# A two-layer fp32 trunk: where the compression weights lie, and in what order the first row tile's attention and the last projections run

## The chip, the cores and the metric

The kernel runs on one core of one Trainium2 chip. The metric is the device time of one execution in microseconds; the time of a kernel is the median of its runs.

## The reference

The input is one sequence of 256 rows with 1024 columns. Two layers follow each other, each of the form `x <- x + RMSNorm_post(mixer(RMSNorm_pre(x)))`. The first mixer is gated linear attention; the change does not touch it. The second is native sparse attention. Cut to what matters here:

```python
p = h @ w_in                       # q 1024, kc, vc, ks, vs, kw, vw 256 each, gates 48, z 1024
q, kc, ks, kw = rope(q), rope(kc), rope(ks), rope(kw)
flat = blocks_of_32_rows(kc or vc) + pe             # 15 overlapping blocks per group
kcmp = silu(flat_k @ ck_w1) @ ck_w2                 # (2048 -> 256 -> 64), the compression
vcmp = silu(flat_v @ cv_w1) @ cv_w2
o = sigmoid(gl + b_gate) * [softmax(q kcmp) vcmp, softmax(q ks) vs, softmax(q kw) vw]
y = (sum of the three) * silu(z) @ w_out
```

There are 16 heads in 4 groups of 4, with 64 columns each. With 256 rows the selection takes every block and the window covers every row, so both those branches are causal attention over all rows.

## The kernel before

**Tiles and precision.** The 256 rows are two row tiles, t = 0 and t = 1, of 128. A projection's weights come in a `Chunk` of 512 (or 280) columns: `load` fetches it in four pieces of 256 rows by 512 columns into buffers named `raw`, of which there are four, and `split` makes of each piece a high part `hi` (ScalarE, line 190) and a low part `lo` (line 196, on VectorE or on GpSimd by a table). A product `mm3` is then three matmuls (lines 211 to 213): high by high, low by high, high by low. The activations are split in the same way into `hT`.

**The second layer, in the order written.** `kc_part(t)` and `ks_part(t)` project kc with vc and ks with vs; the kc side goes through `rope` (VectorE lines 823 and 825, then a GpSimd sum that writes each head twice, `dup`, line 832), is transposed on TensorE and lands in `kcT` (line 850). Line 885 adds the position vectors `vT` to `kcT` and writes `flat`, the compression's input: eight additions, four for kc and four for vc, each one group with all sixteen row positions. `vT` itself is the transpose of `vecs`, made at line 815 before the first `kc_part`. The compression's first weight has eight pieces `w1`, pieces 0 and 1 in the tile later used for z, and pieces 2 to 7 each in a `raw` buffer. `hidden(u)` (lines 891 to 895) runs the eight products of pieces 2u and 2u+1 into one PSUM bank, `o`; in the trace they stand at line 894. The window part kw, vw and the gates are two chunks of 280 columns, `ch_kw[0]` and `ch_kw[1]`. After the fourth `hidden`, silu (`hid`), two transposes, the second compression weight (lines 1175 and 1179), columns 256 to 272 of `kTh`/`kTl` (the compressed keys) and the block matrix `vblk` (line 1186, four pieces) follow.

**Queries, gates and attention.** `q_steps(p, t)` projects half p of the queries for one row tile and ends with `rope`; `q_T` transposes the result into a `qS` tile, of which there are six. `z_steps(p)` projects half p of z, transposed, into two `acc` banks. A `Unit(g, t)` is the attention of group g for row tile t: `scores` (line 1001, scale and row minimum on VectorE at line 1006, exp on ScalarE at line 1008), `values` (transposes of P at line 1074, copies `pT`, products with vs and vw at line 1088, the compressed part through `pcT` at lines 1094 to 1112), and `finish`, which multiplies with the gate and z. `out_steps(t)` is the output projection of a row tile. In row tile 1 a unit has twice the columns.

**What sets the order.** All loads go through one queue in the order written (line 125). The matmuls of projections follow each other on TensorE in the order written (`chain`), and a scheduler places the rest between them by its own model; the pace given to `split` and the numbers `PA[..]` only tell that scheduler beside which matmul a split is to stand. PSUM has two `acc` banks, three `s`, two `t` and one `o`.

In `before` the order after kw is: q(0,0), hidden(2), q_T(0,0), q(0,1), hidden(3), compression's end, q_T(0,1), q(1,0), q(1,1), units (0,0) and (1,0), z(0), unit (2,0), z(1), unit (3,0), out_steps(0), the four units of row tile 1, out_steps(1).

Of the kernel before, what the change touches and what calls it, by code (L numbers as in the profile page):

```python
# [16 lines left out]
P = 128  # L17
# [70 lines left out]
def hybrid_kernel(ctx: ExitStack, tc: tile.TileContext, x, positions, pre_norm, post_norm,  # L88
# [725 lines left out]
    b = bank()  # L814
    nc.tensor.transpose(b[:, :32], vecs, ident[:32, :32])
    nc.vector.tensor_copy(vT, b[:, :32])
# [50 lines left out]
    def load_w1(u0, u1):  # L867
        first = lp.tile([P, 2, 4, CHID], F32, tag="zT", name="w1_0") if u0 == 0 else None
        for u in range(u0, u1):
            raw = wp.tile([P, 4, CHID], F32, tag="raw", name=nm("w1"), bufs=N_RAW) if first is None else first[:, u]  # L870
            src = (nsa_ck_w1, nsa_cv_w1)[u % 2]
            dma(raw, src[0, (u // 2) * 512:(u // 2 + 1) * 512, :].rearrange("(k p) n -> p k n", p=P))
            w1.append(raw)
# [5 lines left out]
    ch_kw[0].load()  # L879
    kc_part(1)  # L880
    for kv in range(2):
# [9 lines left out]
    def hidden(u):  # L891
        for j in range(u * 4, u * 4 + 4):
            for kv in range(2):
                nc.tensor.matmul(hid_b[kv * 64:(kv + 1) * 64, :CHID], flat[:, j, kv].rearrange("p g c -> p (g c)"),  # L894
                                 w1[u * 2 + kv][:, j % 4, :], start=(j == 0), stop=(j == 15))

    ch_kw[0].split((ch_ks, PA[6]))
    for t in range(NT):
        o = proj(ch_kw[0], hT, t)
        nc.scalar.activation(vw_sb[:, t, :24], o[:, 256:280], AF.Copy, scale=rs1[t])  # L900
        k_T(o, t, 272 + t * P)
    hidden(0)
    ch_kw[1].load().split((ch_kw[0], PA[7]))
    load_w1(2, 4)
# [9 lines left out]
    hidden(1)  # L914
# [233 lines left out]

    ch_q[0].load().split((ch_kw[1], PA[8]))
    load_w1(4, 6)  # L1150
    ch_q[1].load(0, 4)
    run(q_steps(0, 0))
    ch_q[1].split((ch_q[0], PA[9]))
    hidden(2)
    load_w1(6, 8)
    ch_q[1].load(4, 8).split((ch_q[0], PA[9]))
    q_T(0, 0)
    q01 = q_steps(0, 1)
    run(q01)
    hidden(3)  # L1160
# [28 lines left out]
    run(q01)  # L1189
# [9 lines left out]

    q_T(0, 1)  # L1200
    run(q_steps(1, 0))
    run(q_steps(1, 1))
    q_T(1, 0)
    unit(0, 0)
    q_T(1, 1)
    unit(1, 0)
    ch_z[0].load().split((ch_q[1], PA[10]))
    run(z_steps(0))
    for g in range(2):
        U[g, 0].finish()  # L1210
    unit(2, 0)
    ch_z[1].load().split((ch_z[0], PA[11]))
# [42 lines left out]
```

## Time and profile before

| | us |
|---|---|
| runs | 307.58, 305.57, 305.70 |
| median | 305.70 |
| profiled execution | 302.72 |
| its span | 300.8 |

The profile shows one execution. Its span runs from the first instruction to the last; the execution's own time is 1.92 us more. The busy time of an engine is the time in which it had an instruction under way: TensorE's matmuls are pipelined, so the length printed for one matmul is longer than the distance to the next. PE is TensorE, PEld its loading of weights, DVE VectorE, ACT ScalarE, POOL GpSimd. In a timeline "x8" counts instructions that stand together in a row, and the bracket at its end is the idle time of the engine just before, with what ended it. A product in fp32 is two passes in the trace, so the eight products of a `hidden` are sixteen matmul records. PEclk is the clock granted to TensorE, 1.00 for 2.4 GHz and 0.50 for 1.2 GHz.

### The profile page before, as it was taken

To read this page: it belongs to the slowest core of one execution; us is meant where nothing else is said; L and a number is where in the kernel's file an instruction comes from. 1 tells how busy PE (TensorE), PEld (TensorE's weight loads), DVE (VectorE), ACT (ScalarE), POOL (GpSimd) and SP (SyncE) were. 2 spreads that over 40 slices of the span, in tenths; PEclk is the share of its full clock that TensorE was granted. 3 is DMA by queue.
4 is the path that set the end of the run, shared out by engine and by line. 5 is a ranking of instruction groups with operands and counts; after the bars stand their busy time and mean duration, and the time that the engine had idled before them with its cause. 6 is when DMAs were issued, how large, how long until landed. Compare 5 with 4: busy or idle time off the path is not lost.

```text
span 300.8 us, 5374 instructions
## 1 busy us (share of the span) xinstructions
PE 286.6 (95%) x1788; PEld 239.7 (80%) x1788; DVE 215.3 (72%) x556; ACT 181.5 (60%) x468; POOL 167.0 (56%) x184
## 2 busy tenths in 40 slices
PE   7999999999999999889979999999997999999991
PEld 7888999999998887668958676899994678676660
DVE  1779569846979877576893536799999858877423
ACT  4896788667754757435534405679967637657301
POOL 1496968984383252927545035897799434172200
PEclk9999999999999999999999999999997799999998
DMA  7997588105677334394745785576144000100001
GB/s 214 403 362 217 151 258 288 56 22 186 204 220 212 92 82 130 64 289 147 195 162 144 274 263 180 190 218 232 42 142 139 2 0 0 71 2 0 2 0 71
DMA packets 28301, 44.57 MB, mean 148 GB/s; under 512 B 2865, under 2 KB 12513, under 8 KB 28274
## 3 DMA queue, kind: packets, MB, share of 16 engines
q1 hardware_dynamic: 28242, 44.23, 46.6%
q8 instruction: 14, 0.23, 0.3%
q14 instruction: 13, 0.11, 0.1%
q10 hardware_dynamic: 32, 0.01, 0.0%
HBM read 43.18 MB, written 1.05 MB: 147 GB/s over the span
## 4 chain that ended last, share of the span: by engine, by line
PE 63%; DVE 13%; issue 9%; POOL 6%; ACT 4%; DMA 3%; SPq 0%; POOLq 0%; DVEq 0%; ACTq 0%
PE acc L211 11%; PE acc L213 11%; PE acc L212 11%; PE s L468 4%; POOL lo L196 3%; PE s L212 3%; PE s L211 3%; PE s L213 3%; DVE lo L196 3%; PE o L894 3%; PE t L1074 3%; PE o L1088 3%; PE s L1001 2%; ACT hi L190 2%; DMA raw<-in_gla_w_in_dram 1%
## 5 line engine op out<-in xcount | busy, mean ns | idle before, releaser
L196 POOL TENSOR_TENSOR lo<-raw,hi 128x512 fp32r<-128x512 f32 (+2 forms) x63 | 82.8, 1334 | 44.4 <-ACT hi L190 44.4
L190 ACT ACTIVATE hi<-raw 128x512 fp32r<-128x512 f32 (+2 forms) x120 | 64.2, 583 | 37.7 <-DMA raw<-in_nsa_w_in_dram 26.6
L196 DVE TENSOR_TENSOR lo<-raw,hi 128x512 fp32r<-128x512 f32 (+2 forms) x57 | 53.6, 963 | 13.4 <-ACT hi L190 13.3
L1045 POOL TENSOR_SCALAR P<-P,cf 128x128 f32<-128x128 f32 (+1 forms) x64 | 29.2, 475 | 30.2 <-DVE cf L1041 14.4
L211 PE MATMUL acc<-hT,hi 128*128 128x256 f32 x160 | 45.2, 283 | 0.1
L212 PE MATMUL acc<-hT,hi 128*128 128x256 f32 x160 | 44.8, 280 | 0.0
L213 PE MATMUL acc<-hT,lo 128*128 128x256 f32 x160 | 44.5, 281 | 0.0
L211 PE MATMUL acc<-hi,hT 128*128 128x512 f32 (+2 forms) x112 | 39.2, 350 | 1.2 <-DVE yg L276 0.8
L213 PE MATMUL acc<-hi,hT 128*128 128x512 f32 (+2 forms) x112 | 38.9, 347 | 0.0
L212 PE MATMUL acc<-lo,hT 128*128 128x512 f32 (+2 forms) x112 | 38.8, 346 | 0.0
L1008 ACT ACTIVATE P<-P,mn 128x128 f32<-128x128 f32 (+1 forms) x64 | 28.4, 445 | 7.2 <-DVE mn L1006 5.9
L211 PEld LDWEIGHTS acc<-hT,hi 128*128 128x128 f32 x160 | 30.1, 188 | 0.4 <-DVE zT L362 0.3
L212 PEld LDWEIGHTS acc<-hT,hi 128*128 128x128 f32 x160 | 30.1, 188 | 0.1
L213 PEld LDWEIGHTS acc<-hT,lo 128*128 128x128 f32 x160 | 29.8, 188 | 0.0
L211 PEld LDWEIGHTS acc<-hi,hT 128*128 128x128 f32 x112 | 21.1, 188 | 5.3 <-ACT yg L269 1.2
L1006 DVE CUSTOM_DVE_ANT_0 P<-s,c 128x128 f32<-128x128 f32 (+1 forms) x64 | 20.6, 347 | 5.3 <-PE s L1001 4.4
L213 PEld LDWEIGHTS acc<-hi,hT 128*128 128x128 f32 x112 | 21.1, 188 | 2.9 <-DVE hT L311 0.4
L212 PEld LDWEIGHTS acc<-lo,hT 128*128 128x128 f32 x112 | 21.1, 188 | 2.0
L1074 PE MATMUL t<-c,P 128*128 128x128 f32 x96 | 17.4, 296 | 2.0 <-ACT pcT L1096 1.9
L440 POOL TENSOR_TENSOR lo<-raw,hi 128x512 fp32r<-128x512 f32 (+1 forms) x9 | 12.3, 1388 | 9.9 <-ACT hi L436 9.8
L1074 PEld LDWEIGHTS t<-c,P 128*128 128x128 f32 x96 | 11.1, 147 | 7.3 <-issue 3.6
L832 POOL TENSOR_TENSOR dup<-rt,rt 128x512 f32<-128x512 f32 x6 | 8.9, 1487 | 11.2 <-DVE rt L825 5.7
(268 smaller groups left out, 676.2 us busy)
## 6 DMA issues: line engine op xcount, KB each, us to landing
raw<-in_nsa_w_in_dram SPq DMA_DIRECT2D x24, 512.0 KB, 4.5
raw<-in_gla_w_in_dram SPq DMA_DIRECT2D x12, 512.0 KB, 6.1
raw<-in_gla_w_out_dram SPq DMA_DIRECT2D x8, 512.0 KB, 4.3
raw<-in_nsa_w_out_dram SPq DMA_DIRECT2D x8, 512.0 KB, 4.2
raw<-in_nsa_w_in_dram SPq DMA_DIRECT2D x8, 280.0 KB, 8.4
raw<-in_gla_w_in_dram SPq DMA_DIRECT2D x6, 344.0 KB, 3.4
home<-in_gla_w_in_dram SPq DMA_DIRECT2D x4, 512.0 KB, 6.7
w<-in_nsa_ck_w_dram SPq DMA_DIRECT2D x4, 512.0 KB, 3.8
```

What stands on the lines that cost most here:

```text
L190: m = after(nc.scalar.activation(hi[:, j, :n], raw[:, j, :n], AF.Copy), prev)
L196: eng.tensor_sub(lo[:, j, :n], raw[:, j, :n], f(hi[:, j, :n]))
L211: m = nc.tensor.matmul(o, a[0], b[0], start=start, stop=False, **kw)
L212: nc.tensor.matmul(o, a[0], b[1], start=False, stop=False, **kw)
L213: return m, nc.tensor.matmul(o, a[1], b[0], start=False, stop=stop, **kw)
L440: line(e, eng.tensor_sub(lo[:, j, :n], raw[:, j, :n], f(hi[:, j, :n])))
L468: m = nc.tensor.matmul(o[t][:, :chunk.n], hT[i][:, k, t * P:(t + 1) * P], w[j], start=(k == b == 0), stop=(k == KT - 1 and b == 2))
L894: nc.tensor.matmul(hid_b[kv * 64:(kv + 1) * 64, :CHID], flat[:, j, kv].rearrange("p g c -> p (g c)"), w1[u * 2 + kv][:, j % 4, :], start=( ...
L1006: nc.vector.tensor_tensor_reduce(out=o, in0=src, in1=masks[br], op0=ALU.add, op1=ALU.min, scale=-0.125, scalar=3.0e38, accum_out=self.mn[: ...
L1008: nc.scalar.activation(o, o, AF.Exp, scale=-1.0, bias=self.mn[:, j:j + 1], accum_out=self.sm[:, j:j + 1])
L1045: nc.gpsimd.tensor_scalar(o, o, cf[:, i * 2 + br:i * 2 + br + 1], 1.0, op0=ALU.mult, op1=ALU.mult)
L1074: pe(nc.tensor.transpose(b[:, i * P:(i + 1) * P], self.Pt[i][:, c0:c0 + P], ident))
```

## The change

The position vectors' transpose and copy move from before `kc_part(0)` to behind `kc_part(1)`. Pieces 2 to 7 of `w1` go into the six `qS` tiles, which are empty until the first `q_T`, and no longer into `raw`; so they are loaded ahead: pieces 2 and 3 before `kc_part(1)`, pieces 4 to 7 before the kw projections, together with `ch_kw[1]` and `ch_q[0]`. `hidden(1)` and `hidden(2)` follow the two row tiles of kw1, `hidden(3)` comes right after, and all their matmuls are now in the chain. The compression's end then lies beside q(0,0) and q(0,1). Behind it the order is: q(0,1), unit (0,0), z(0), unit (1,0), q(1,0), finish of both, q(1,1), unit (2,0), z(1), unit (3,0).

```diff
--- before.py
+++ after.py
@@ -811,9 +811,6 @@
     flat = cp.tile([P, 16, 2, GROUPS, 16], F32, tag="flat", name="flat")
     nc.gpsimd.memset(flat, 0.0)
     vT = cp.tile([P, 32], F32, tag="vT", name="vT")
-    b = bank()
-    nc.tensor.transpose(b[:, :32], vecs, ident[:32, :32])
-    nc.vector.tensor_copy(vT, b[:, :32])
 
     def rope(o, nh, t, twice):
 
@@ -865,9 +862,10 @@
     w1 = []
 
     def load_w1(u0, u1):
         first = lp.tile([P, 2, 4, CHID], F32, tag="zT", name="w1_0") if u0 == 0 else None
         for u in range(u0, u1):
-            raw = wp.tile([P, 4, CHID], F32, tag="raw", name=nm("w1"), bufs=N_RAW) if first is None else first[:, u]
+            raw = lp.tile([P, 4, CHID], F32, tag="qS", name=nm("w1"), bufs=6) if first is None else first[:, u]
             src = (nsa_ck_w1, nsa_cv_w1)[u % 2]
             dma(raw, src[0, (u // 2) * 512:(u // 2 + 1) * 512, :].rearrange("(k p) n -> p k n", p=P))
             w1.append(raw)
@@ -877,7 +875,11 @@
     ch_z = [Chunk(w_in, N_Z + p * 512, 512) for p in range(2)]
     load_w1(0, 2)
     ch_kw[0].load()
+    load_w1(2, 4)
     kc_part(1)
+    b = bank()
+    nc.tensor.transpose(b[:, :32], vecs, ident[:32, :32])
+    nc.vector.tensor_copy(vT, b[:, :32])
     for kv in range(2):
         kin = kcT[:, kv]
         for g in range(GROUPS):
@@ -891,17 +893,21 @@
     def hidden(u):
         for j in range(u * 4, u * 4 + 4):
             for kv in range(2):
-                nc.tensor.matmul(hid_b[kv * 64:(kv + 1) * 64, :CHID], flat[:, j, kv].rearrange("p g c -> p (g c)"),
-                                 w1[u * 2 + kv][:, j % 4, :], start=(j == 0), stop=(j == 15))
+                m = nc.tensor.matmul(hid_b[kv * 64:(kv + 1) * 64, :CHID], flat[:, j, kv].rearrange("p g c -> p (g c)"),
+                                     w1[u * 2 + kv][:, j % 4, :], start=(j == 0), stop=(j == 15))
+                chain(m, m)
 
     ch_kw[0].split((ch_ks, PA[6]))
+    ch_kw[1].load()
+    load_w1(4, 8)
+    ch_q[0].load()
     for t in range(NT):
         o = proj(ch_kw[0], hT, t)
         nc.scalar.activation(vw_sb[:, t, :24], o[:, 256:280], AF.Copy, scale=rs1[t])
         k_T(o, t, 272 + t * P)
+        if t == 0:
+            ch_kw[1].split((ch_kw[0], PA[7]))
     hidden(0)
-    ch_kw[1].load().split((ch_kw[0], PA[7]))
-    load_w1(2, 4)
     for t in range(NT):
         o = proj(ch_kw[1], hT, t)
         nc.scalar.activation(vw_sb[:, t, 24:], o[:, :232], AF.Copy, scale=rs1[t])
@@ -911,7 +917,10 @@
         nc.scalar.activation(g, g, AF.Exp, scale=-1.0)
         nc.vector.tensor_scalar(g, g, 2.0, 2.0, op0=ALU.mult, op1=ALU.add)
         nc.vector.reciprocal(g, g)
-    hidden(1)
+        hidden(t + 1)
+        if t == 0:
+            ch_q[0].split((ch_kw[1], PA[8]))
+    hidden(3)
 
 
 
@@ -1146,18 +1155,8 @@
             sl = slice(n * H, n * H + H)
             dma(out[0, t * P:(t + 1) * P, sl], X[:, t, sl])
 
-    ch_q[0].load().split((ch_kw[1], PA[8]))
-    load_w1(4, 6)
-    ch_q[1].load(0, 4)
-    run(q_steps(0, 0))
-    ch_q[1].split((ch_q[0], PA[9]))
-    hidden(2)
-    load_w1(6, 8)
-    ch_q[1].load(4, 8).split((ch_q[0], PA[9]))
-    q_T(0, 0)
-    q01 = q_steps(0, 1)
-    run(q01)
-    hidden(3)
+    q00 = q_steps(0, 0)
+    run(q00, 3)
     zT = lp.tile([P, KT, S], F32, tag="zT", name="zT2")
     hid = cp.tile([P, CHID], F32, tag="hid", name="hid")
     silu2(hid_b[:, :CHID], hid)
@@ -1186,7 +1185,8 @@
             nc.vector.tensor_tensor(vblk[:, 2 * p + G], b[rows, (p + 1) * 64:(p + 2) * 64].unsqueeze(1)
                                     .to_broadcast([64, 4, DH]),
                                     cc("blk")[rows].unsqueeze(2).to_broadcast([64, 4, DH]), op=ALU.mult)
-    run(q01)
+    run(q00)
+    q_T(0, 0)
     l2a.close()
     ap_ = ctx.enter_context(tc.tile_pool(name="l2b", bufs=1))
     ofT = [[lp.tile([P, KT, P], F32R, tag="qS", name=nm("ofT"), bufs=6) for n in "hl"] for t in range(NT)]
@@ -1197,19 +1197,21 @@
         run(U[g, t].scores())
         run(U[g, t].values())
 
+    ch_z[0].load().split((ch_q[0], 8))
+    run(q_steps(0, 1))
+    unit(0, 0)
     q_T(0, 1)
+    run(z_steps(0))
+    ch_q[1].load().split((ch_z[0], 0))
+    unit(1, 0)
     run(q_steps(1, 0))
-    run(q_steps(1, 1))
-    q_T(1, 0)
-    unit(0, 0)
-    q_T(1, 1)
-    unit(1, 0)
-    ch_z[0].load().split((ch_q[1], PA[10]))
-    run(z_steps(0))
     for g in range(2):
         U[g, 0].finish()
+    q_T(1, 0)
+    ch_z[1].load().split((ch_q[1], 0))
+    run(q_steps(1, 1))
     unit(2, 0)
-    ch_z[1].load().split((ch_z[0], PA[11]))
+    q_T(1, 1)
     run(z_steps(1))
     unit(3, 0)
     for g in range(2, 4):
```

The instructions' order on the engines, as the two programs have them, at three places.

VectorE around the additions `flat`, in the window projections; `lo` are splits of kw weights, `acc` is the bank of kw's first chunk, row tile 0, and `cos_t`, `sin_t` mark its rope. Before:

```order
L196 TENSOR_TENSOR lo_1939<-raw_1922,hi_1938 128x280
L850 COPY kcT<-t_1732 64x4x64
L850 COPY kcT<-t_1739 64x4x64
L885 TENSOR_TENSOR flat<-kcT,vT 128x16x15 x4
L196 TENSOR_TENSOR lo_1945<-raw_1924,hi_1944 128x280
L885 TENSOR_TENSOR flat<-kcT,vT 128x16x15 x4
L823 TENSOR_TENSOR rt_324_1856<-acc_1830,cos_t 128x256
L825 TENSOR_TENSOR rt_325_1857<-acc_1830,sin_t 128x4x32 x2
L338 COPY rb<-t_1795 128x256
```

And after:

```order
L196 TENSOR_TENSOR lo_1917<-raw_1840,hi_1916 128x280
L847 COPY kcT<-t_1733 64x4x64
L847 COPY kcT<-t_1740 64x4x64
L820 TENSOR_TENSOR rt_338_1884<-acc_1858,cos_t 128x256
L822 TENSOR_TENSOR rt_339_1885<-acc_1858,sin_t 128x4x32 x2
L882 COPY vT<-t_1747 128x32
L887 TENSOR_TENSOR flat<-kcT,vT 128x16x15 x8
L338 COPY rb<-t_1799 128x256
```

The rope of kw0's row tile 0 now stands ahead of the eight additions, and the copy `vT` between them, which waits for a transpose of TensorE.

That transpose and the first `hidden` on TensorE; `acc_1922` is kw0's row tile 1, `acc_1970` kw1's row tile 0, `dup_1789` belongs to ks. After:

```order
L211 MATMUL acc_1922<-hi_1828,hT_1317 128x280
L881 MATMUL t_1747<-c_64,vecs 128x32
L212 MATMUL acc_1922<-lo_1829,hT_1317 128x280
L213 MATMUL acc_1922<-hi_1828,hT_1318 128x280
L836 MATMUL t_1791<-c_64,dup_1789 128x128 x4
L211 MATMUL acc_1922<-hi_1828,hT_1317 128x280
L212 MATMUL acc_1922<-lo_1829,hT_1317 128x280
L213 MATMUL acc_1922<-hi_1828,hT_1318 128x280
L337 MATMUL t_1799<-dg_1803,onesr 128x256
L337 MATMUL t_1799<-dg_1804,onesr 128x256
L896 MATMUL o_1798<-w_0_1684,flat 64x256 x8
L211 MATMUL acc_1970<-hi_1898,hT_1317 128x280
```

Before the change line 894 stood at the same place, behind the same projection, and the transpose of `vecs` ahead of the layer's first projection.

TensorE at the end of q(0,1) and the start of the next projection; `t_2195` and `t_2101` are the bank with the compressed keys and values, `acc_2309`, `acc_2310` the two banks of z(0), and `acc_2185` the bank of q(0,1), whose buffer `acc_2310` takes over. Before:

```order
L211 MATMUL s_2257<-hi_2122,hT_1317 128x512
L1175 MATMUL t_2195<-hidT,w_1580 128x64 x2
L1179 MATMUL t_2195<-w_1580,hidR 128x64 x4
L963 MATMUL t_2216<-c_64,rt_384_2169 128x128 x4
L212 MATMUL s_2257<-lo_2123,hT_1317 128x512
...
L213 MATMUL s_2257<-hi_2128,hT_1318 128x512
L211 MATMUL acc_2506<-hT_1317,hi_2482 128x256
```

And after:

```order
L212 MATMUL acc_2185<-lo_2027,hT_1317 128x512
L1174 MATMUL t_2101<-hidT,w_1580 128x64 x2
L1178 MATMUL t_2101<-w_1580,hidR 128x64 x4
L213 MATMUL acc_2185<-hi_2026,hT_1318 128x512
L211 MATMUL acc_2185<-hi_2026,hT_1317 128x512
L212 MATMUL acc_2185<-lo_2027,hT_1317 128x512
L213 MATMUL acc_2185<-hi_2026,hT_1318 128x512
L211 MATMUL acc_2309<-hT_1317,hi_2161 128x256
...
L972 MATMUL t_2135<-c_64,rt_369_2129 128x128 x4
...
L211 MATMUL acc_2310<-hT_1317,hi_2161 128x256
```

VectorE at that place, after:

```order
L296 TENSOR_TENSOR kTl<-t_2101,kTh 128x4x16
L1185 TENSOR_TENSOR vblk<-t_2101,c_65 64x256 x4
L820 TENSOR_TENSOR rt_390_2210<-acc_2185,cos_t 128x512
L822 TENSOR_TENSOR rt_391_2211<-acc_2185,sin_t 128x8x32 x2
```

Before, the bank of q(0,1) was an `s` bank; now it is the `acc` bank that z(0) needs six of its matmuls and four transposes after the end of q(0,1), and its rope stands behind `kTl` and the four `vblk`.

TensorE after the last matmul of z(1) (the first row in both pieces); `P` are the probabilities, `s` the score banks, `acc_2996` is the first bank of out_steps(0). Before:

```order
L213 MATMUL acc_2736<-hT_1317,lo_2730 128x256
L1001 MATMUL s_2846<-kTh,qS_2293 128x272
...
L1074 MATMUL t_2457<-c_64,P_2395 128x128 x2
L1074 MATMUL t_2457<-c_64,P_2418 128x128 x2
L1088 MATMUL o_2022<-pT_2455,vs_sb 64x256 x2
L1094 MATMUL t_2466<-c_64,cS_2393 64x128
L1074 MATMUL t_2679<-c_64,P_2624 128x128 x2
...
L1088 MATMUL o_2022<-pT_2462,vw_sb 64x256 x2
L1112 MATMUL o_2022<-pcT_2468,vblk 128x128 x2
...
L211 MATMUL acc_2996<-hi_2934,ofT_2212 128x512
```

And after:

```order
L213 MATMUL acc_2736<-hT_1317,lo_2606 128x256
L1010 MATMUL s_2655<-kTh,qS_2574 128x272
...
L1010 MATMUL s_2678<-kTl,qS_2574 128x272
L211 MATMUL acc_2996<-hi_2934,ofT_2149 128x512
L212 MATMUL acc_2996<-lo_2935,ofT_2149 128x512
L213 MATMUL acc_2996<-hi_2934,ofT_2150 128x512
...
L211 MATMUL acc_2997<-hi_2958,ofT_2149 128x512
L1010 MATMUL s_2846<-kTh,qS_2574 128x272
...
L213 MATMUL acc_2997<-hi_2958,ofT_2150 128x512
L1083 MATMUL t_2701<-c_64,P_2646 128x128 x2
```

Before, the transposes and products of units (1,0) (`P_2395`, `P_2418`) and (2,0) (`P_2624`, `P_2647`) follow the scores of (3,0) directly. Now units (0,0) and (1,0) are done before z(1) ends; what stands there are three quarters of the scores of (2,0) (`s_2655` to `s_2678`), 24 matmuls of the output projection, with scores of (3,0) between the last of them, and then the transposes of (2,0).

## Rows read from the trace of the kernel before

**Rows 1.** The page: its first line, and busy time by engine.
```profile
span 300.8 us, 5374 instructions
PE 286.6 (95%) x1788; PEld 239.7 (80%) x1788; DVE 215.3 (72%) x556; ACT 181.5 (60%) x468; POOL 167.0 (56%) x184
```

**Rows 2.** PE's waits from 110 to 260 us: total, times, longest.
```profile
PE t L1074 <- ACT pcT L1096: 1.8, 1, 1.8
PE o L894 <- DVE flat L885: 1.6, 1, 1.6
```

**Rows 3.** Windows: busy us by engine, then PEclk, DMA share, GB/s.
```profile
150.00:155.00 5.00, 3.43 (x27) 2.36 (x27) 4.97 (x13) 2.00 (x4) 0.58 (x1) 1.00 0.80 270
...
225.00:230.00 5.00, 3.13 (x23) 2.19 (x22) 4.91 (x19) 3.51 (x11) 5.00 (x8) 0.97 0.62 211
230.00:235.00 5.00, 5.00 (x20) 3.69 (x21) 5.00 (x12) 3.17 (x11) 3.42 (x3) 0.50 0.01 2
235.00:240.00 5.00, 5.00 (x28) 2.99 (x27) 4.23 (x23) 3.73 (x14) 2.50 (x6) 0.85 0.01 3
```

**Rows 4.** Timeline of PE: the compression's first products, and two matmuls of q.
```profile
151.26 0.65 PE L894 MATMUL o<-w,flat 128*64 128x256 f32 x2
153.48 2.81 PE L894 MATMUL o<-w,flat 128*64 128x256 f32 x24 [1.57 <-DVE flat L885]
...
170.26 0.65 PE L894 MATMUL o<-w,flat 128*64 128x256 f32 x2
...
171.17 0.39 PE L212 MATMUL acc<-lo,hT 128*128 128x512 f32 x1
171.40 0.40 PE L213 MATMUL acc<-hi,hT 128*128 128x512 f32 x1
```

**Rows 5.** Timeline of DVE, 145 to 154 us; the first row from a narrower window.
```profile
145.60 1.54 DVE L196 TENSOR_TENSOR lo<-raw,hi 128x280 fp32r<-128x280 f32 x1
...
148.93 2.18 DVE L885 TENSOR_TENSOR flat<-kcT,vT 128x240 f32<-128x240 f32 x4
151.04 0.43 DVE L196 TENSOR_TENSOR lo<-raw,hi 128x280 fp32r<-128x280 f32 x1
151.40 2.02 DVE L885 TENSOR_TENSOR flat<-kcT,vT 128x240 f32<-128x240 f32 x4
153.45 0.42 DVE L823 TENSOR_TENSOR rt<-acc,cos_t 128x256 f32<-128x256 f32 x1
153.79 0.48 DVE L825 TENSOR_TENSOR rt<-acc,sin_t 128x128 f32<-128x128 f32 x2
154.19 0.41 DVE L338 COPY rb<-t 128x256 f32<-128x256 f32 x1
```

**Rows 6.** Timeline of POOL, 145 to 147 us.
```profile
145.34 1.49 POOL L832 TENSOR_TENSOR dup<-rt,rt 128x512 f32<-128x512 f32 x1 [2.10 <-DVE lo L196]
```

**Rows 7.** Timeline of PE, 129 to 131 us: the transpose of `vecs`.
```profile
129.94 0.24 PE L815 MATMUL t<-c,vecs 32*128 32x32 f32 x1 [0.71 <-DVE xg L307]
```

**Rows 8.** Timeline of PE after z(1).
```profile
230.00 1.09 PE L1074 MATMUL t<-c,P 128*128 128x128 f32 x4 [1.79 <-ACT pcT L1096]
```

**Rows 9.** Timeline of PE at the compression's end.
```profile
191.46 0.55 PE L1175 MATMUL t<-hidT,w 128*128 128x64 f32 x4
191.85 1.06 PE L1179 MATMUL t<-w,hidR 128*128 128x64 f32 x8
```

**Rows 10.** Timeline of DVE at the end of q(0,1).
```profile
195.26 0.69 DVE L823 TENSOR_TENSOR rt<-s,cos_t 128x512 f32<-128x512 f32 x1 [1.99 <-PE s L213]
195.87 0.74 DVE L825 TENSOR_TENSOR rt<-s,sin_t 128x256 f32<-128x256 f32 x2
196.53 0.21 DVE L296 TENSOR_TENSOR kTl<-t,kTh 128x64 fp32r<-128x64 f32 x1
196.66 1.71 DVE L1186 TENSOR_TENSOR vblk<-t,c 64x256 f32<-64x256 f32 x4
```

**Rows 11.** Timeline of DVE in the attention of row tile 1.
```profile
245.62 0.43 DVE L1006 CUSTOM_DVE_ANT_0 P<-s,c 128x256 f32<-128x256 f32 x1 [3.29 <-PE s L1001]
```

## The prediction

> **What bounds the kernel now.** I read the page's busy times first. TensorE has 286.6 of the span's 300.8 us and the next engine, VectorE, 215.3 [rows 1]: what doesn't shorten TensorE's work or one of its pauses gains nothing on average. So the second view is TensorE's list of waits in the stretch that the change touches, 110 to 260 us, and there are only two that count: 1.8 us for the copy `pcT` of a unit of row tile 0 and 1.6 us for the additions `flat` [rows 2]. The third view is the windows around these two places. At 150 to 155 us VectorE is busy 4.97 of 5 us while TensorE has 3.43, at clock 1.00. At 225 to 230 us VectorE has 4.91 and GpSimd all 5.00 while TensorE has 3.13; then the clock is 0.50 for the whole window 230 to 235, and 0.97 and 0.85 in the neighbours [rows 3]. At the half level the stretch is 0.03 x 5 / 0.5 = 0.3 us, 5 us, and 0.15 x 5 / 0.5 = 1.5 us, together 6.8 us. The wait ahead of that stretch is 1.79 us [rows 8]; the wait of 1.57 us for `flat` [rows 4] was followed by no fall. The two are nearly the same length, so the clock at either place can tip. The kernel is thus bound by TensorE, with one place, behind z(1), where VectorE and GpSimd hold it up and cost it the clock too.
>
> **The change part by part.** The sum is made against the profiled execution, 302.72 us (span 300.8 and 1.92 around it), which is 2.98 us under the median 305.70; the result is put on the median by adding that.
>
> *Where w1 lies.* The bytes are the same; they come earlier, in buffers that nothing else uses then. The trace shows no wait of TensorE for a load in this stretch [rows 2], and the transfers have 0.80 of the engines' time where the kw pieces and w1 are fetched [rows 3]. So nothing is gained in time by fetching ahead, and I cost it at 0. The cover is the projection of kc and kw. On the queue the four last pieces of w1 now stand ahead of q's first chunk; if that came late, TensorE would wait at q(0,0), and I keep this in the upper end of the range.
>
> *A. The transpose of `vecs` leaves its old place.* There it ran 0.24 us in a pause of 0.71 that was a wait for the normalised input [rows 7]; that input is still waited for. Gain at most 0.3, and I book it in B.
>
> *B. The additions.* VectorE does eight additions in 2.18 + 2.02 us, 4.2 together, from 148.93 to 153.42, with one split of 0.43 between, and the first `hidden` waits for the last of them [rows 4, 5]. Now the rope of kw0 comes first: from 153.45 to 154.19 before, so 0.74 us [rows 5]. Then `vT` waits for its transpose, which stands on TensorE five matmuls, four transposes and the two small row-scale products ahead of `hidden`: five at 0.23 x 280 / 512 = 0.13 [rows 4] and, as an estimate, 1 us for the six small ones (the twelve records of rows 9 took 1.45) put it near 149.6, counted back from 151.26. With 0.24 for it and 0.2 for the copy the additions can start near 150.1; the rope, behind one split more (0.43), ends at 148.9 + 0.4 + 0.7 = 150.0. Both limits agree. Eight additions end at 154.4 undisturbed, 1.0 us later than before; less A's 0.3 this is +0.7. But the rope's end also releases GpSimd's `dup`, which took 1.49 us, and while it ran the split on VectorE took 1.54 us where the same form takes 0.43 [rows 5, 6], 1.1 more. If the additions suffer likewise, B is +1.8. I take +1.5, nearer to the row of the split, with +0.4 to +2.8 as ends (the lower if the transpose runs a little earlier, the upper if the next GpSimd split slows them too).
>
> The Trainium skill (page "SBUF — State Buffer", section "SBUF: two separate sides") says that a VectorE operation with two inputs in SBUF and a GpSimd operation share a port pair under an exclusive lock. The split in rows 5 beside the `dup` in rows 6 agrees with it; no row of before shows an addition `flat` beside a GpSimd operation. By this rule B would be +1.8 and the sum 0.3 higher; without it B is +0.7 and the sum 0.8 lower.
>
> *C. The clock behind it.* The four additions of kc end near 152.2 to 153.3, the four of vc near 154.4 to 155.5; TensorE is there at 151.0. It would wait some 1.3 to 2.3 us, do one product of 0.3, and wait again 1.8. That is more idling than the 1.79 us that went before the half clock at 229.7 [rows 3, 8] and much more than the 1.57 that cost nothing. I think a fall likely. Its price: 6.8 us at half speed lose 3.4 us where TensorE is the bound, nothing where it waits; kw1 follows, which is pure matmul, so 2.6 as the likeliest, 0 to 3.4 the bounds.
>
> *D. Fewer changes between the two kinds of matmul.* A pair of passes that stands alone between projections took 0.65 us, and 24 in a row took 2.81, or 0.12 each [rows 4]: a stretch of its own costs 0.65 - 0.23 = 0.4 us. In before the 64 passes stand in seven stretches, now in four. Three times 0.35: -1.0, between 0 and -1.3.
>
> *E. The wait behind z(1) goes.* Units (0,0) and (1,0) now end before z(1) does, and 24 matmuls of the output projection, at 0.23 us each [rows 4] 5.6 us, stand where TensorE had only transposes and products of two units with VectorE's and ScalarE's copies between them. So the 1.79 us of waiting [rows 8] and the 3.4 us of the half clock [rows 3] go: 5.2 at most, 5.0 taken. Late next there is VectorE with the scores of units (2,0) and (3,0), see G.
>
> *F. The values of unit (0,0)* wait behind z(0) for a copy on the engines that evacuate z(0); nothing in before shows this; 0 to +1, +0.4 taken.
>
> *H. z(0)'s second bank.* It takes over the bank of q(0,1), which VectorE's rope must have read. The rope stands behind `kTl` and four `vblk`. From the start of the second compression product: 0.4 + 1.06 on TensorE [rows 9], about 0.2 for the high part, 0.2 for `kTl`, 1.71 for `vblk`, then 0.6 + 0.7 for the rope [rows 10], 4.9 us. TensorE meanwhile does those products, four matmuls of q(0,1), six of z(0) and four transposes, 3.4 us. +1.5, between 0 and +2.
>
> *G. VectorE behind z(1).* It was busy 4.91 and 5.00 of 5 us in the two windows from 225 [rows 3], and in the attention of row tile 1 it then had a pause of 3.29 us, waiting for TensorE [rows 11]. That pause was TensorE's half clock and the output projection between the units. 5.6 us of that filler are now used earlier. With its own slack of 3.29 against 5.6, VectorE can be 2.3 us late at the worst, and the late units of row tile 0 add to it: 0 to +4, +1.5 taken, nearer to the pause than to its absence.
>
> The sum: B +1.5, C +2.6, D -1.0, E -5.0, F +0.4, H +1.5, G +1.5 = +1.5. 302.7 + 1.5 = 304.2, on the median 307.2 us.
>
> **The rivals.** A measurement of this kernel tells about 1%, 3.1 us, from no change.
>
> *The clock stays.* The additions end early (B +0.7) and the first `hidden`s wait too little for a fall: C is 0 and the sum 0.7 - 1.0 - 5.0 + 0.4 + 1.5 + 1.5 = -1.9: 303.8 us. If G is nothing as well, 302.3; if H is too, 300.8. For it: 1.57 us of waiting left the clock at 1.00 [rows 3, 4]. Against it: the additions stand in a longer row of work than before, on an engine that was already busy 4.97 of 5.
>
> *VectorE becomes the bound in row tile 1, and the clock falls there (slower).* The filler that TensorE had between the units of row tile 1 is used up before them. If VectorE is behind by more than its pause of 3.29 us [rows 11] once the 24 matmuls are over, TensorE idles between transposes and products, about 4 us, and loses 3.3 more to a half-clock stretch like that from 229.7. G is then 4 + 3.3 instead of 1.5: 307.2 + 5.8 = 313.0 us. For it: VectorE is full at 225 to 235 [rows 3]. Against it: the softmax and copies of units (0,0) and (1,0) are then over, which they were not before.
>
> *The change doesn't do what it says.* The wait behind z(1) stays, because the scores of (2,0) and (3,0) hold the banks: E is 0, and 307.2 + 5.0 = 312.2 us. Against it: in the order the 24 matmuls need only z(1) and finished units.
>
> **How the numbers follow.** Forecast (B, C and E as summed) 0.45, with a range of its own from 304.5 to 310.0; the clock stays 0.35; VectorE as the bound 0.13; the wait stays 0.07. Under 302.6 lies nearly half of the second case and a little of the first: 0.18 for faster. Over 308.8 lie a third of the first, all of the third, nearly all of the fourth: 0.15 + 0.13 + 0.06 = 0.34 for slower. The rest is 0.48. The range from 301.8 to 311.8 leaves out the best corner of the second case, most of the third and half of the fourth, together 0.2.
>
> **What would show it.** Right: in the profile after, the first product of the compression waits twice for `flat`, together over 2.5 us, at a clock that reads about half in the next window; the copy `vT` waits for TensorE; the second bank of z(0) waits over 1 us for the rope; behind z(1) no wait over 0.5 us for `pcT`, and clock 1.00. Wrong: one wait for `flat` under 1.6 us with the clock at 1.00 in the window after it puts the time near 303.8; a clock under 0.9 between 230 and 260 us puts it near 313; a wait of TensorE for a load anywhere in kw or q, or any new one over 2 us in units of row tile 1, would mean that a part that I cost at little carries the result.

## The result, and the profile after

The changed kernel takes 308.32 us (median of 15 runs, 307.51 to 309.14), the kernel before 305.15 us (15 runs, 302.54 to 307.58): a ratio of 1.0123, with a 95% interval of 1.0097 to 1.0148. It is slower by a little more than the 1% that the prediction took as the bound, though the interval reaches just under it. The ratios here and below leave out executions that took over 1.5% longer than the fastest of their kernel (three of e10's twelve, one of e8's, single ones of before), and the medians keep them. The forecast, 307.2 us, is 1.1 us too low, and the time lies in the range.

The page of the changed kernel: its first line, busy time by engine, and the granted clock in 40 slices.

```profile
span 306.1 us, 5372 instructions
...
PE 286.4 (94%) x1788; PEld 239.1 (78%) x1788; DVE 220.3 (72%) x556; ACT 180.6 (59%) x468; POOL 167.8 (55%) x184
...
PEclk9999999999999999999969999999999999999999
```

TensorE is busy for as long (286.4 us against 286.6 [rows 1]) in a span 5.3 us longer. The profiled execution of before, 302.72 us, was one of its shorter ones; that of after, 307.91, is near its median. So the medians differ by 3.2 us and the spans by 5.3, and a sum over rows has to explain the 5.3.

TensorE's waits from 110 us on (total, times, longest):

```profile
PE o L896 <- DVE flat L887: 5.0, 2, 2.8
PE acc L211 <- DVE rt L822: 1.5, 1, 1.5
PE s L1010 <- DVE mn L1015: 1.3, 1, 1.3
...
PE acc L213 <- DVE hT L311: 0.7, 1, 0.7
PE o L1097 <- ACT pT L1087: 0.6, 1, 0.6
```

The wait for `pcT` of [rows 2] is gone. The wait for `flat` is 5.0 us in two pieces where it was 1.6 in one, and there is a wait of 1.5 for a rope, and one of 1.3 for a row minimum. The windows show what followed (busy us by engine, PEclk, DMA share, GB/s):

```profile
150.00:155.00 5.00, 2.76 (x19) 2.26 (x18) 4.93 (x11) 2.30 (x5) 2.60 (x2) 0.97 1.07 390
155.00:160.00 5.00, 2.19 (x10) 0.90 (x10) 5.00 (x9) 3.08 (x6) 2.13 (x2) 0.50 0.31 120
160.00:165.00 5.00, 5.00 (x34) 3.92 (x31) 5.00 (x5) 0.60 (x1) 4.70 (x3) 0.84 0.45 117
...
235.00:240.00 5.00, 5.00 (x25) 4.17 (x24) 5.00 (x20) 4.85 (x19) 3.80 (x3) 1.00 0.12 46
250.00:255.00 5.00, 3.52 (x23) 2.18 (x23) 4.87 (x22) 3.96 (x14) 1.88 (x4) 1.00 0.00 0
```

Against [rows 3] the two places have changed roles. Behind z(1), which now ends at 234.8 us, the clock reads 1.00 throughout. The half clock now stands at the waits for the additions: from 154.7 us, when the first of them ends, over the second and the products behind it, 0.03 x 5 / 0.5 + 5 + 0.16 x 5 / 0.5 = 6.9 us long, as long as the old one. The timeline of TensorE shows both waits, and the one at z(0)'s second bank:

```profile
154.66 1.07 PE L896 MATMUL o<-w,flat 128*64 128x256 f32 x2 [2.24 <-DVE flat L887]
158.53 3.42 PE L896 MATMUL o<-w,flat 128*64 128x256 f32 x14 [2.81 <-DVE flat L887]
...
190.84 0.36 PE L211 MATMUL acc<-hT,hi 128*128 128x256 f32 x1 [1.53 <-DVE rt L822]
```

The first two of the sixteen passes wait 2.24 us, the other fourteen 2.81 more; in [rows 4] the second group waited 1.57 and nothing else did. The fourteen then take 3.42 us at half clock. VectorE at that place, the last three rows from narrow windows:

```profile
149.80 0.77 DVE L847 COPY kcT<-t 64x256 f32<-64x256 f32 x2
...
152.10 1.51 DVE L887 TENSOR_TENSOR flat<-kcT,vT 128x240 f32<-128x240 f32 x1
...
154.51 1.54 DVE L887 TENSOR_TENSOR flat<-kcT,vT 128x240 f32<-128x240 f32 x1
155.98 1.52 DVE L887 TENSOR_TENSOR flat<-kcT,vT 128x240 f32<-128x240 f32 x1
```

And GpSimd:

```profile
151.57 1.68 POOL L829 TENSOR_TENSOR dup<-rt,rt 128x512 f32<-128x512 f32 x1 [2.11 <-DVE vT L882]
154.08 3.05 POOL L196 TENSOR_TENSOR lo<-raw,hi 128x512 fp32r<-128x512 f32 x2 [0.83 <-ACT hi L190]
```

Eight additions last from 151.56 to 158.5, 6.9 us, and 4.2 in [rows 5]. They are not slow evenly: five take about 0.6 us, as before, and three take 1.5. Three operations of GpSimd run beside them, one `dup` and two splits. The splits are those of the first query chunk. Its first piece has not come earlier than in before, as ScalarE's high parts show, which wait for it (the first row is of before, the second of after):

```profile
153.13 1.15 ACT L190 ACTIVATE hi<-raw 128x512 fp32r<-128x512 f32 x2 [1.48 <-DMA raw<-in_nsa_w_in_dram]
153.37 1.15 ACT L190 ACTIVATE hi<-raw 128x512 fp32r<-128x512 f32 x2 [0.77 <-DMA raw<-in_nsa_w_in_dram]
```

In before the additions were over at 153.42 [rows 5], and GpSimd came to the first of these splits at 155.66, behind a `dup`:

```profile
155.66 1.27 POOL L196 TENSOR_TENSOR lo<-raw,hi 128x512 fp32r<-128x512 f32 x1
```

So it is the additions that have moved, into the time of the splits.

### The profile page after: what moved, and what is told of

Read it like the earlier page. It is cut to its first block, busy times and chain, and to the rows that moved or that the text cites. A ratio compares the mean times of both kernels' runs of the same rounds, so it can differ in the third digit from the quotient of the medians.

```text
span 306.1 us, 5372 instructions
## 1 busy us (share of the span) xinstructions
PE 286.4 (94%) x1788; PEld 239.1 (78%) x1788; DVE 220.3 (72%) x556; ACT 180.6 (59%) x468; POOL 167.8 (55%) x184
## 4 chain that ended last, share of the span: by engine, by line
PE 67%; DVE 14%; issue 7%; ACT 5%; POOL 3%; DMA 2%; SPq 0%; POOLq 0%; DVEq 0%; ACTq 0%
PE acc L211 12%; PE acc L213 12%; PE acc L212 12%; PE s L468 4%; PE s L211 3%; PE s L212 3%; PE s L213 3%; DVE lo L196 3%; PE o L896 3%; PE o L1097 3%; PE t L1083 2%; PE s L1010 2%; ACT P L1017 2%; DVE flat L887 2%; DMA raw<-in_gla_w_in_dram 2%
## 5 line engine op out<-in xcount | busy, mean ns | idle before, releaser
L196 POOL TENSOR_TENSOR lo<-raw,hi 128x512 fp32r<-128x512 f32 (+2 forms) x63 | 85.2, 1378 | 45.5 <-ACT hi L190 45.4
L190 ACT ACTIVATE hi<-raw 128x512 fp32r<-128x512 f32 (+2 forms) x120 | 62.9, 581 | 17.8 <-DMA raw<-in_nsa_w_in_dram 6.1
L196 DVE TENSOR_TENSOR lo<-raw,hi 128x512 fp32r<-128x512 f32 (+2 forms) x57 | 56.3, 1012 | 11.0 <-ACT hi L190 10.7
L1054 POOL TENSOR_SCALAR P<-P,cf 128x128 f32<-128x128 f32 (+1 forms) x64 | 27.8, 454 | 27.8 <-DVE cS L1064 7.6
L1083 PE MATMUL t<-c,P 128*128 128x128 f32 x96 | 18.4, 284 | 0.0
L1010 PE MATMUL s<-kTh,qS 128*128 128x272 f32 (+1 forms) x48 | 15.8, 339 | 1.6 <-DVE mn L1015 1.3
```

What stands on the lines that cost most here:

```text
L190: m = after(nc.scalar.activation(hi[:, j, :n], raw[:, j, :n], AF.Copy), prev)
L196: eng.tensor_sub(lo[:, j, :n], raw[:, j, :n], f(hi[:, j, :n]))
L1010: pe(nc.tensor.matmul(o, q[i], k[:, g, c0:c1], start=(m == 0), stop=(m == 1)))
L1054: nc.gpsimd.tensor_scalar(o, o, cf[:, i * 2 + br:i * 2 + br + 1], 1.0, op0=ALU.mult, op1=ALU.mult)
L1083: pe(nc.tensor.transpose(b[:, i * P:(i + 1) * P], self.Pt[i][:, c0:c0 + P], ident))
```

## The experiments

All times are medians; the kernel before ran on the same chip with each group (304.12 us beside e1 to e4, 303.92 beside e5 to e8, 303.64 beside e9 and e10). The groups ran on different chips, so between groups the ratios to before, or two traces, say more than the medians do.

**e1_vt_early: the transpose and copy of `vT` back at their old place.**

```diff
     vT = cp.tile([P, 32], F32, tag="vT", name="vT")
+    b = bank()
+    nc.tensor.transpose(b[:, :32], vecs, ident[:32, :32])
+    nc.vector.tensor_copy(vT, b[:, :32])
...
     kc_part(1)
-    b = bank()
-    nc.tensor.transpose(b[:, :32], vecs, ident[:32, :32])
-    nc.vector.tensor_copy(vT, b[:, :32])
```

> The changed kernel with the transpose and copy of vT back ahead of the first kc_part; the order then puts the eight additions ahead of kw0's rope, and with the rope GpSimd's dup and two splits stand behind them. Theory (the additions are slowed by GpSimd's operations beside them): they start near 150.6, take 4.2 to 4.6 us instead of 6.92, the first hidden's wait falls from 5.0 to about 2.5 us, and the clock may stay: 303.7 to 306.0 us. Rival (only the late start counts): they start 1.0 us earlier and still take 6.9: about 307.3 us.

Measured: 302.48 us, a ratio to before of 0.9943 (0.9911 to 0.9975), 5.8 us under the changed kernel by the medians and 5.5 by the two ratios; that is 1.2 us under the expected range. The additions (ns of one, minimum, median, maximum; first and last start), TensorE's waits, and the windows:

```profile
L887 DVE TENSOR_TENSOR flat<-kcT,vT x8: 570/577/618, 149.5 to 153.0; 128x240 f32<-128x240 f32 x8
```

```profile
PE o L896 <- DVE flat L887: 2.0, 2, 1.3
PE acc L211 <- DVE rt L825: 1.5, 1, 1.5
```

```profile
150.00:155.00 5.00, 2.96 (x23) 1.84 (x22) 4.97 (x13) 0.88 (x2) 0.46 (x1) 1.00 1.07 393
155.00:160.00 5.00, 5.00 (x38) 4.07 (x36) 3.44 (x6) 4.57 (x9) 4.31 (x4) 1.00 0.41 156
```

With an empty GpSimd the longest addition is 0.62 us, and the eight take from 149.5 to 153.55. That goes with the theory; the rival wanted 6.9 us. The start came earlier too, by 2 us, so the two still had to be parted. The traces say where the gain lies: from kw's first product to the end of the last `hidden` the changed kernel takes 31.0 us (144.16 to 175.19) and this one 25.7 (143.03 to 168.77), and from there to the end both take 130.9.

The runs of this kernel also say something of the clock's price. In six of twelve the mean granted clock over the span was 0.997 or 0.998, in three 0.987 or 0.988, and in the other three between. The mean times of the first two groups are 302.0 and 304.0. A mean lower by 0.01 is 6 us of the 300 at half clock, one such stretch, and it goes with 2.0 us. Where it stood in those runs their records don't say, nor whether a longer wait ahead of it is part of the 2.0.

**e4_rope_behind: `vT` late as in the change, but kw0's rope ordered behind the last addition.**

```diff
-        nc.vector.tensor_mul(t1[:, :nh], ov, CSt[:, t].unsqueeze(1).to_broadcast([P, nh, 2, HD]))
+        m = nc.vector.tensor_mul(t1[:, :nh], ov, CSt[:, t].unsqueeze(1).to_broadcast([P, nh, 2, HD]))
+        after(m, behind)
...
-            nc.vector.tensor_add(flat[:, :, kv, g, :NCMP], src,
+            last_flat = nc.vector.tensor_add(flat[:, :, kv, g, :NCMP], src,
...
-        k_T(o, t, 272 + t * P)
+        k_T(o, t, 272 + t * P, last_flat)
```

> The changed kernel with kw0's rope of row tile 0 ordered behind the last addition; vT stays late. GpSimd then has one split beside the additions instead of the dup and two splits. Theory: the additions start near 151.2 as in the changed kernel and take 4.2 to 5.5 us instead of 6.92; the wait is 2.5 to 3.5 us instead of 5.0: 305 to 307 us. Rival (the additions are slow by themselves in this place): they take over 6.5 us and the time is 308 us or more.

Measured: 303.84 us (ratio to before 0.9984, 0.9952 to 1.0016), under the expected range as well.

```profile
L888 DVE TENSOR_TENSOR flat<-kcT,vT x8: 576/582/618, 151.2 to 154.7; 128x240 f32<-128x240 f32 x8
```

```profile
155.00:160.00 5.00, 4.63 (x35) 3.80 (x36) 3.81 (x11) 4.17 (x8) 3.80 (x3) 1.00 0.56 195
```

The additions start at 151.2, as late as in the changed kernel (151.6), and none is slow. The wait for them is 2.2 us, and the window behind it reads 1.00; in five of the twelve runs the mean clock was 0.988 or 0.989, so they had a stretch at half clock that the profiled execution hasn't. Most of e1's gain is so recovered without moving `vT`: 4.5 us by the medians, and from kw's first product to the last `hidden` 26.0 us in the trace where the changed kernel has 31.0 and e1 25.7 (the clock's part is in that). What moving `vT` adds, 1.4 us, is the smaller part. GpSimd's split that I expected beside the additions ran behind them: the query piece that it needs is waited for until 155.50 in this trace, 2.1 us later than in the changed kernel, and the additions end at 155.3.

**e7_dup_alone: the first splits of the query chunk on VectorE, behind the additions.**

In the table that names the splits for GpSimd, the entry of that chunk:

```diff
-(0, 2, 3, 5)
+(4, 5, 6, 7)
```

> The changed kernel with the first splits of q's first chunk moved from GpSimd to VectorE, behind the additions; beside the eight additions GpSimd then has only kw0's dup of 1.7 us. Theory (each GpSimd operation with SBUF operands slows VectorE while it runs): the additions take 5.5 to 6.0 us, between 4.6 with nothing beside them and 6.92; the wait falls by about 1.2 us and the time to 306.5 to 307.5. Rival (only the dup counts): 6.9 us and 308.3.

Measured: 307.14 us (ratio to before 1.0112, 1.0084 to 1.0141). The additions, then GpSimd, then VectorE's four splits behind the additions:

```profile
L887 DVE TENSOR_TENSOR flat<-kcT,vT x8: 558/576/1506, 152.1 to 156.5; 128x240 f32<-128x240 f32 x8
```

```profile
152.10 1.68 POOL L829 TENSOR_TENSOR dup<-rt,rt 128x512 f32<-128x512 f32 x1 [2.10 <-DVE vT L882]
158.92 3.38 POOL L829 TENSOR_TENSOR dup<-rt,rt 128x512 f32<-128x512 f32 x1 [5.14 <-DVE rt L822]
```

```profile
158.67 2.48 DVE L196 TENSOR_TENSOR lo<-raw,hi 128x512 fp32r<-128x512 f32 x4
```

One GpSimd operation beside the additions, one addition of 1.5 us, and 152.09 to 157.1 for the eight: 5.0 us, less than the expected 5.5 to 6.0. With three it was three additions and 6.9, with none it is none and 4.1. Each operation of GpSimd costs VectorE about 1.0 us. The time itself is 1.2 us under the changed kernel's by the medians, but the two ratios don't part them (1.0112 and 1.0123). It also works the other way: the second `dup` met four splits of VectorE without a gap, and took 3.38 us where [rows 6] have 1.49.

**e5_fill: matmuls that nobody reads in the two waits.** 18 and 22 of them, into an `s` bank.

```diff
                 chain(m, m)
+                if u == 0 and j == 0 and kv == 0:
+                    idle(22)
+
+    def idle(n):
+        b = bank("s")
+        for i in range(n):
+            m = nc.tensor.matmul(b[:, :S], onesr, hT[0][:, i % KT, :], start=(i == 0), stop=(i == n - 1))
+            chain(m, m)
...
+    idle(18)
     hidden(0)
```

> The changed kernel with 18 and 22 matmuls that nobody reads put into its two waits for the additions, 2.1 and 2.6 us long, so that TensorE goes on working there; they add no work where it would not have waited. Theory (the half clock behind these waits costs about 2.1 us): the clock reads 1.00 from 150 to 165 us and the time is 306.0 to 306.8 us. Rival (the half clock costs nothing, since TensorE mostly waits in it): 308.0 to 308.8 us.

Measured: 307.38 us, 0.9 under the changed kernel by the medians and not 2.1; by the two ratios to before, both 1.0123, it gained nothing. Windows, and two of its waits:

```profile
150.00:155.00 5.00, 5.00 (x41) 4.80 (x40) 4.90 (x10) 1.05 (x3) 2.88 (x3) 1.00 1.05 375
155.00:160.00 5.00, 4.39 (x32) 3.60 (x30) 5.00 (x7) 3.46 (x6) 3.02 (x2) 1.00 0.74 287
160.00:165.00 5.00, 3.91 (x29) 2.98 (x30) 5.00 (x8) 1.63 (x3) 3.16 (x3) 1.00 0.08 11
```

```profile
...
PE t L836 <- DVE kTl L296: 1.5, 1, 1.5
...
PE o L896 <- DVE flat L887: 0.2, 1, 0.2
```

The clock stays at 1.00, as expected. But TensorE then comes earlier to the transposes of kw0's second half, and waits 1.5 us there for VectorE, which is as late as before. From kw's first product to the end the two traces take 162.0 and 161.5 us. So in the changed kernel the half clock alone costs between nothing and 0.9 us, neither what the theory nor quite what the rival said: without it VectorE's lateness shows a little later. (The profiled execution, 309.15 us, is the longest of the six; 1.7 us of that it lost in the first layer, which no edit touches.)

**e2_w1_only and e3_order_only: the two halves of the change apart.** e2 has the compression part with the old order of queries, z and attention, e3 the new order with w1, `vT` and `hidden` as before.

```diff
-    q00 = q_steps(0, 0)
-    run(q00, 3)
+    run(q_steps(0, 0))
+    ch_q[1].load().split((ch_q[0], PA[9]))
+    q_T(0, 0)
+    q01 = q_steps(0, 1)
+    run(q01)
...
-    ch_z[0].load().split((ch_q[0], 8))
-    run(q_steps(0, 1))
+    q_T(0, 1)
+    run(q_steps(1, 0))
+    run(q_steps(1, 1))
+    q_T(1, 0)
     unit(0, 0)
...
```

> Only the compression part of the change (w1 in the query tiles, vT moved, hidden in the chain), queries, z and attention in the order of before. Theory (the loss is in this part): before plus 3.5 of waiting, 2.1 of clock, 0.7 at kc, less 1.0 for fewer switches, near 310.4 us, and the wait behind z(1) is there as before. Rival (the loss is in the new attention order): 305.2 us, no half clock near 155.

Measured: 310.63 us, 6.5 over before (ratio 1.0192, 1.0146 to 1.0237). Its waits:

```profile
PE o L896 <- DVE flat L887: 3.2, 1, 3.2
PE o L1097 <- DVE pT L1089: 3.1, 2, 2.6
PE o L896 <- DMA raw<-in_nsa_w_in_dram: 2.2, 1, 2.2
```

The two rows for `o L896` are the two pieces of the wait for the additions; in the first a load is named, since it landed last before the release. The wait behind z(1) has stayed (2.6 the longest, for `pT`). The theory's 310.4 was right.

```diff
     ch_q[0].load().split((ch_kw[1], PA[8]))
     load_w1(4, 6)
-    ch_q[1].load(0, 4)
     run(q_steps(0, 0))
...
+    ch_z[0].load().split((ch_q[0], 8))
     q01 = q_steps(0, 1)
     run(q01)
...
+    unit(0, 0)
     q_T(0, 1)
+    run(z_steps(0))
+    ch_q[1].load().split((ch_z[0], 0))
+    unit(1, 0)
     run(q_steps(1, 0))
-    run(q_steps(1, 1))
...
```

> Only the new order of queries, z and the units of row tile 0, with w1, vT and hidden as before. Theory (this part gains by itself): no wait behind z(1) and no half clock after it, -5.0, with +1.5 to +3 given back at z(0)'s bank and in row tile 1: 302 to 304 us. Rival (VectorE becomes the bound in row tile 1): over 306 us, with waits of TensorE over 3 us there.

Measured: 313.59 us, 9.5 over before (ratio 1.0292, 1.0234 to 1.0349); the theory expected a gain. Its waits:

```profile
PE s L1001 <- DVE cS L1027: 2.7, 5, 1.3
PE acc L211 <- DVE zT L362: 2.5, 1, 2.5
...
PE s L1001 <- DVE kTl L296: 1.3, 1, 1.3
PE t L1094 <- DVE cs L1057: 1.2, 1, 1.2
```

Neither theory had this. With w1 in the `raw` buffers the fourth `hidden` comes behind q(0,1), so the compressed keys are ready only at the end of z(0). The scores of units (0,0) and (1,0) need them, stand there with only the last 15 matmuls of z(0) between them, and TensorE waits for `kTl` and for VectorE's reading of each score bank; the output projection behind z(1) then waits 2.5 us for a gate of z, and in the order all eight scores of units (2,0) and (3,0) stand behind the first part of it. So the new order costs where the compression ends late; what it is worth where it ends early, e10 tells.

**e10_w1_vt: e2 with e1's edit.**

> Only the compression part with vT early (e2_w1_only with e1's edit), queries, z and attention in the order of before. Against e1's 302.48 it tells what the new order is worth once the compression ends early. Theory (the wait behind z(1) and its half clock go with the order, 5.0, less 1.5 at z(0)'s bank, 0.6 and 1.3 after it): 304.1 us, with the wait for pT or pcT behind z(1) and a clock under 0.9 near it. Rival (the order is worth nothing or costs, as e3_order_only suggests): 302.5 us or less.

Measured: 304.37 us (ratio to before 0.998, 0.9937 to 1.0023).

```profile
PE o L1097 <- DVE pT L1089: 3.6, 1, 3.6
PE o L896 <- DVE flat L887: 2.2, 2, 1.3
```

```profile
155.00:160.00 5.00, 5.00 (x31) 3.46 (x28) 3.79 (x8) 3.45 (x6) 4.02 (x3) 0.75 0.40 154
230.00:235.00 5.00, 2.91 (x13) 1.96 (x14) 4.97 (x18) 3.11 (x10) 4.38 (x4) 0.76 0.04 16
```

Beside e1 this is the price of the new order once its condition holds: 302.48 - 304.37 = -1.9 us, where the prediction's steps for it, E, F, G and H, sum to -1.6. The size is not sure: e10's twelve runs lie between 301.23 and 308.29 us, the two ratios to before make it -1.1, and their intervals overlap. What the traces show is that the wait behind z(1), 3.6 us here, and the half clock behind it go with the order. By itself, the early compression is worth nothing that shows (ratio 0.998). The first of the two windows shows a half clock behind the additions as well, after 2.2 us of waiting; e4's profile had none after the same 2.2.

**e6_bank: e1 with the bank of q(0,1) from `s`.**

```diff
-QB = ('acc', 'acc', 's', 's')
+QB = ('acc', 's', 's', 's')
```

> e1_vt_early with the bank of q(0,1) taken from the s banks in place of acc. Theory (z(0)'s second bank waits 1.5 us for the rope behind kTl and vblk): that wait is gone and the time is 1.5 us under e1's 302.48, near 301.0. Rival (TensorE waits elsewhere instead, for scores or for q_T(0,1)): 302.5 us.

Measured: 301.44 us (ratio to before 0.9928, 0.9901 to 0.9955).

```profile
PE s L1010 <- DVE qS L978: 0.5, 1, 0.5
```

The 1.5 us for the rope are gone; 1.0 of them shows in the medians, and in the traces too (from the last `hidden` to the end 129.9 us against e1's 130.9); 0.5 comes back as a wait for `qS`, a little later, behind the same VectorE.

**e8_later: e6 with the first `hidden` behind kw1's first row tile.**

```diff
-    hidden(0)
...
+        if t == 0:
+            hidden(0)
         hidden(t + 1)
```

> e6_bank with hidden(0) behind the first row tile of kw1 and directly ahead of hidden(1). Theory (the 2.0 us that e1 still waits for the additions are then covered by 24 matmuls of 0.13 us, 3.1 us): no wait for flat, 299.0 us. Rival (kw1's row tile waits for its own splits, or the wait moves to the end of the compression): 301 us, as e6_bank.

Measured: 304.56 us, 3.1 more than e6, which neither side expected (ratio to before 1.002, 0.9995 to 1.0045). Its longest wait and a window:

```profile
PE acc L211 <- DVE rt L825: 3.7, 1, 3.7
```

```profile
155.00:160.00 5.00, 3.81 (x21) 3.84 (x22) 3.47 (x10) 2.30 (x4) 3.12 (x3) 0.75 0.73 282
```

There is no wait for `flat` any more, but one of 3.7 us in its place: kw1's first row tile takes over the `acc` bank of kw0's, and the rope that frees it stands behind the eight additions. In e6 the waits at `hidden(0)` stood ahead of it. The longer single wait brought a half clock too.

**e9_later_s: e8 with kw1's banks from `s`.**

```diff
-        o = proj(ch_kw[1], hT, t)
+        o = proj(ch_kw[1], hT, t, "s")
```

> e8_later with kw1's two banks taken from s, so that its first row tile need not wait for kw0's rope, which stands behind the additions. Theory (e8 lost its gain only to the bank, 3.7 us of waiting and a half clock): no wait for the rope or the additions over 0.5 us, clock 1.00, 299 to 300 us, 1.5 to 2.5 under e6's 301.44. Rival (the next wait, for the split of kw1 or for kTl, takes its place): 301.5 us or more.

Measured: 299.43 us, a ratio to before of 0.9843 (0.9793 to 0.9892).

```profile
PE s L1011 <- DVE mn L1016: 1.6, 2, 1.4
PE t L839 <- POOL dup L832: 0.8, 1, 0.8
```

```profile
150.00:155.00 5.00, 5.00 (x40) 4.78 (x39) 4.94 (x11) 0.88 (x2) 0.00 (x0) 1.00 1.08 385
```

In the window where before had TensorE busy 3.43 of 5 us [rows 3] it now has 5.00, and no wait for the additions or the rope is left. This version is 1.6% faster than before and, by the two ratios to before (0.9843 / 1.0123), 2.8% faster than the change.

## Why the prediction was right, and where its steps were not

The forecast was slower than before by 1.5 us and the medians differ by 3.2: right in sign and in mechanism (a longer wait for the additions, then a half clock, which together eat the gain behind z(1)), too small in one term, B. It gave the class that came, slower by over 1%, a chance of 0.34 only, because it had that term too small. That the time itself is missed by only 1.1 us is in part luck: the median of before, on which the forecast was put, came out 0.55 us lower over more runs, so the rise over before is missed by 1.7; and the sizes of several terms were off in opposite directions.

*A, the transpose of `vecs`:* wrong in sign. The gain was to be up to 0.3 us. In its old place the transpose filled a pause; in its new one four transposes of `dup` slipped into that pause, and a matmul of kc then waits 0.7 us for `hT`. What makes `hT` late is again a GpSimd operation: a `dup` from 130.99 to 132.27 us, with which VectorE's `hT` takes 1.49 us, while without one two of them took 1.37 in before.

```profile
131.33 1.49 DVE L311 TENSOR_TENSOR hT<-xg,hT 128x512 fp32r<-128x512 f32 x1
```

Counted from the end of the first layer, the kc stage takes 0.5 us longer than in before, and than in e1.

*Where w1 lies:* TensorE waits for no load, as costed.

*B, the additions:* the step that was too small. The prediction counted one GpSimd operation beside the additions, the `dup`, at 1.1 us, and left a split to the upper end; there were three operations, at about 1.0 each (e7, e1). The start was also 1.4 us later than worked out (151.56 for 150.1), since `kcT` is copied from 149.8 on, where the additions of before already began at 148.9; five splits stand ahead of it where four stood. Each lateness fed the next: the first query piece landed when it did in before, but now the additions were still running. So the wait for `flat` rose by 2.24 + 2.81 - 1.57 = 3.5 us and not by 1.5. That is 0.7 over the upper end that was given for B. No run holds the splits back and leaves everything else; e7 moves them to another engine. The Trainium skill's rule (page "SBUF — State Buffer", section "SBUF: two separate sides") holds here in its strict form: a VectorE addition with two inputs in SBUF and a GpSimd operation do not share, one waits for the other, 0.57 us against 1.5. The row of before that the prediction set it beside (1.54 against 0.43) shows the same.

*C, the clock:* came as forecast, with 6.9 us at half clock. The fourteen passes behind the second wait took 3.42 us where in before fourteen took 1.94 (the row from 172.19 us), and the two ahead of it 1.07 for 0.65: 1.9 us of TensorE's time. e1's two groups of runs give 2.0. That is under the 2.6 taken and inside its bounds.

```profile
172.19 1.94 PE L894 MATMUL o<-w,flat 128*64 128x256 f32 x14
```

As a price of the kernel it is smaller still as long as B stands: filling the waits returned at most 0.9 (e5), because VectorE was late behind them.

*D, fewer stretches of `hidden`:* right. The 64 passes took 9.3 us of TensorE's time in seven stretches in before, without the wait, and 8.2 in four stretches in e1 at full clock: -1.1 for -1.0.

*E, the wait behind z(1):* right that it goes. No `pcT` row is left, and the clock reads 1.00 in every window there. Its 5.2 us were not measured alone; e10 tests only the sum of E to H, and that roughly.

*F, H, G:* 0.6 us for 0.4, 1.5 for 1.5, 1.3 for 1.5 (the waits for `pT` at `L1097`, for the rope, for the row minimum). For E, F, G and H together e10 gives -1.1 to -1.9; the steps gave -1.6.

With these sizes (E's as the prediction had it at most): A +0.5, B +3.5, C +1.9, D -1.1, E -5.2, F +0.6, H +1.5, G +1.3 make +3.0 us. The medians differ by 3.2 and the two spans by 5.3. What is left of the latter lies in TensorE's busy time and not in its waits: the span less the busy time is 14.2 us in before and 19.7 in after, +5.5, which is about what B, F, H, G, A's wait and the 1.8 of E's make; but C, D and the 3.4 of E's half clock should have taken 2.6 us off the busy time, and it fell by 0.2. Counted from each start to the next, the transposes of `dup` take 0.7 us more than in before, the scores with `kTh` 0.6 and the transposes of `cS` 0.5. Why, no experiment here has told.

*A mistake in the text ahead of the prediction.* The piece of before's order that stands beside the end of q(0,1) is the end of q(1,1), and the rope of [rows 10] and the small products of [rows 9] are those beside q(1,1). The bank of q(0,1) is an `acc` bank in both programs. What the change does is to put z(0) directly behind q(0,1). The durations, and with them H, do not depend on this.

*The rivals.* "The clock stays" did not come, "VectorE becomes the bound in row tile 1" came in a small form (one wait of 1.34 us, clock 1.00), "the wait stays" not at all in the whole change, though e2 and e10 show that it does without the new order.

## What to carry to other kernels

A piece of work that is moved later meets what falls due in the meantime: before costing the move at its length, look which loads land then, where the conversions that they release will run, and beside what. When work is put on VectorE between a producer and a waiting TensorE, count the GpSimd operations that will run at the same time, about one full operation each. And before filling a wait with the next projection, check which bank that projection takes over and who has to read it first: e8 lost 3.1 us to that, and one word for the bank (e9) made it the best version.

## What the hardware showed that was not expected

GpSimd and VectorE delayed each other by whole operations: 0, 1 and 3 GpSimd operations beside eight additions gave 0, 1 and 3 additions of 1.5 us among others of 0.57 (e1, e7, the changed kernel), and a `dup` of GpSimd stretched to 3.38 us beside four splits of VectorE. And executions of one program (e1) differed by one stretch at half clock, and with it by 2.0 us, with the same order and the same work; in the profiles, waits for the additions of 2.2 us in all were followed by one in e10 and by none in e4.
